# The right-hand end of SBUF at 229280 instead of 229344 in an encoder layer with windowed attention and a SwiGLU feed-forward

## The chip, the cores and the metric

The kernel runs on one core of a Trainium2 chip. The metric is the device time of one execution in microseconds; the time before is the median of three runs.

The core has five engines with queues of their own: TensorE (PE, with its weight loads listed as PEld), VectorE (DVE), ScalarE (ACT), GpSimd (POOL) and SyncE (SP), which here issues nearly all DMAs. SBUF holds the operands, 128 partitions wide; an address below is a byte offset within each partition. PSUM holds the matmul results in eight banks.

## What is computed

One layer (`DEPTH = 1`) of a bidirectional encoder on a 2048 x 1024 sequence in float32: windowed grouped-query attention with 16 query and 4 key heads, then a SwiGLU feed-forward part of 2816 hidden columns. Both are wrapped in norms and in shift, scale and gate vectors that come from a conditioning vector `c`:

```python
mod = (c_act @ ada_w[i] + ada_b[i])[:, None, :]
sh1, sc1, g1, sh2, sc2, g2 = jnp.split(mod, 6, axis=-1)
h = rmsnorm(x, mix_norm_pre[i]) * (1.0 + sc1) + sh1
y = windowed_gqa_sink(h, att_w_qkv[j], att_w_o[j], att_sink[j], rel_bias)
x = x + g1 * rmsnorm(y, mix_norm_post[i])
h = rmsnorm(x, ffn_norm_pre[i]) * (1.0 + sc2) + sh2
y = swiglu(h, ffn_w_in[i], ffn_w_out[i])
x = x + g2 * rmsnorm(y, ffn_norm_post[i])
```

## The kernel before

**Arithmetic.** Every large product is taken as three matmuls (`three`): an operand is split into a rounded half `hi` (a copy to the type fp32r, on ACT) and a rest `lo` (a subtraction, on DVE or POOL), and hi x hi, hi x lo and lo x hi are added up in one PSUM bank. A moving operand has 512 columns in most of these matmuls, the loaded one 128 x 128.

**Stages.** First the modulation products (`ada_reduce`, DVE, each over a 512 KB tile of `ada_w`) together with the first chunk's norm and the query, key and value products of 512 tokens at a time. Then attention in 64 units of a 128-query block and a key head: scores, softmax in the tiles `pr`, transposes by PE with the identity matrix (`ident`), and values. The remaining query, key and value products and the output projections (`OProj`) are woven in between the units. The last chunk's output projection follows by itself. Then come the two products of the feed-forward part. Both use a scheme with seven block products for a 2 x 2 block product (`Block.STEPS`): seven combinations of weights (`a11, s2, a12, s3, s1, a22, s4`) are multiplied with seven operands (`b11, t2, b21, t3, t1, t4, b22`). In the first part (`Hidden`, 44 blocks of seven steps with 12 matmuls each) the blocks' weights take turns between two pools, `wi0` and `wi1`. In the second part (`Outs`) most steps have nine matmuls. The end of the second part is done without the scheme, with operands `gls` and weights `wl`. In the trace `ht...` are operands whose name begins with t, `hb...` those that begin with b, `wa_i` and `ws_i` the weights of the first part, `wa_o` and `ws_o` those of the second.

**Order.** The program is not written straight to the chip. `Recorder` records about 15,700 operations with the buffers they read and write. `place` then gives each pool an address. Pools opened with `side="left"` are stacked upwards from `SBUF_LEFT = 1152`, those with `side="right"` downwards from `SBUF_RIGHT`, and a closed pool gives its room to the next on its side. `forward` and `backward` plan the order of each engine by fixed costs and choose a buffer for each tile. Addresses enter the plan only through `t.earlier` and `t.later`, the lists of earlier buffers whose bytes a buffer overlaps. `emit` issues the planned order with the planned addresses.

**Where the operands lie.** The two sides of the main pools:

| pool | side | bytes from | holds |
|---|---|---|---|
| const | left | 1152 | `mod`, `nsink`, `ones`, `ident` |
| xs, nrm, hs, ev | left | 2560 | activations of the query, key and value products, conditioning row `cb` |
| constr | right | 228864 | `adab`, `gains`, `epsc`, `coef`: 192 + 128 + 32 + 128 bytes |
| w2, raws, w1 | right | 110080 | their weights, raw and split; the `ada_w` tiles |
| bp, qkv, ptp, ob, ws, sm | right | 124160 | attention: bias, q, k, v, phi, plo, output, woven weights |
| pp | right | 105632 | softmax tiles `pr`, three buffers of 6176 bytes |
| op, yp | left | 2560 | output projection of chunks 0 to 2: operands, results |
| op3, wop3, yp3 | right | 148992 | the same for chunk 3, with its weights |
| wi0, hA, b21, t3 | left | 2560 | first part: half of the blocks' weights, operands b11, t2, b21, t3, t1 |
| wi1, hB, tmp | right | 128512 | first part: the other blocks' weights, operands t4, b22, hidden values |
| wo, hA2, tmpo | left | 2560 | second part: all weights, operands b11, t2 |
| hB2, y3 | right | 89600 | second part: operands b21, t3, t1, t4, b22, running sums `z` |

The tiles are 2048 or 4096 bytes in most pools. Those of attention are 1024 to 8192, the weights of the second part 1536 to 6144; all of these are multiples of 256. Not so are the small constants and statistics and `pr`: a buffer of `pr` holds four heads of 385 numbers, 1540 bytes apart.

**Lines.** All operations are issued at line 586 (`emit`), so the profile tells them apart by tile names. The change is in line 68.

Of the kernel before, what the change touches and what calls it, by code (L numbers as in the profile page):

```python
# [64 lines left out]


SBUF_LEFT = 1152
SBUF_RIGHT = 229344
BANKS = 8
BANK = 2048  # L70

# [58 lines left out]
class Recorder:  # L130
# [139 lines left out]
    def place(self):  # L270


        at = {"left": SBUF_LEFT, "right": SBUF_RIGHT, "psum": 0}
        stack = {k: [] for k in at}
# [1379 lines left out]
```

## Time and profile before

| | us |
|---|---|
| median of three runs | 2086.82 |
| lowest and highest run | 2083.96, 2087.82 |
| the profiled execution | 2096.39 |
| its span, first to last instruction | 2094.6 |
| PE busy in it | 2012.7 |
| DVE busy | 1649.6 |
| ACT busy | 1069.9 |
| POOL busy | 755.9 |

The profiled execution is one execution with the profiler on. Its rows add up to its own time, not to the median. A row of a group of instructions gives the engine, the operation, the tiles written and read (out<-in; for a matmul the moving operand first, the loaded one second), the shapes, the count, then busy us and mean ns of one, and the idle time before them with what ended it. Matmuls overlap with their successors, so the time from one start to the next is shorter than the mean of one. The share of DMA is the mean busy share of the core's 16 DMA engines.

### The profile page before, as it was taken

The page shows a single profiled execution, that of the slowest core. Times are in us where ns is not written, and L with a number is a line of the kernel's source. Part 1 is how long each engine was busy: PE and PEld are TensorE (multiplying, and loading weights), DVE is VectorE, ACT ScalarE, POOL GpSimd, SP SyncE. Part 2 cuts the span into 40 slices and gives each one's busy share as a digit, 9 for nine tenths or more (in the row PEclk, how much of TensorE's full clock was granted, in tenths as well). Part 3 has the DMA queues.
Part 4 walks back from the last instruction along what each step waited for, and adds up shares of the span by engine and source line. Part 5 has one row for each costly group of instructions (what it writes and reads, how often), then busy time and mean ns, then how long its engine had stood idle before and what let it go on. Part 6 is the DMA issues. An engine that isn't in the chain of part 4 may idle for free. (4 is left out here: it accounts for less than half of the span.)

```text
span 2094.6 us, 29028 instructions
## 1 busy us (share of the span) xinstructions
PE 2012.7 (96%) x9366; PEld 1664.9 (79%) x9366; DVE 1649.6 (79%) x2933; ACT 1069.9 (51%) x2122; POOL 755.9 (36%) x687
## 2 busy tenths in 40 slices
PE   5899999999999989999999999999999999998997
PEld 4687788888778768888888888888888888876886
DVE  7657777765557879977788897786666789998998
ACT  4447666677777865343433442233333744465432
POOL 2403544456888823543454332222221000240040
PEclk9999999999999999999999999999999999999999
DMA  8887755676768695545456844432233544447553
GB/s 298 266 274 238 234 180 187 209 234 230 237 226 279 207 351 187 187 137 172 158 156 212 288 148 164 133 126 101 94 108 121 181 153 139 146 129 246 168 163 106
DMA packets 200516, 396.35 MB, mean 189 GB/s; under 512 B 20091, under 2 KB 62124, under 8 KB 195244
## 3 DMA queue, kind: packets, MB, share of 16 engines
q1 hardware_dynamic: 199788, 393.97, 56.3%
q8 instruction: 74, 1.21, 0.2%
q14 instruction: 78, 0.64, 0.1%
q10 hardware_dynamic: 576, 0.52, 0.1%
HBM read 270.65 MB, written 123.76 MB: 188 GB/s over the span
## 5 line engine op out<-in xcount | busy, mean ns | idle before, releaser
L586 PE MATMUL bank<-ht,ws_i 128*128 128x512 f32 x1584 | 373.5, 389 | 0.0
L586 PEld LDWEIGHTS bank<-ht,ws_i 128*128 128x128 f32 x1584 | 297.2, 188 | 62.1 <-DVE p_i L586 0.5
L586 PE MATMUL bank<-hb,wa_i 128*128 128x512 f32 x1056 | 253.6, 389 | 0.7 <-DVE u_i L586 0.7
L586 PEld LDWEIGHTS bank<-hb,wa_i 128*128 128x128 f32 x1056 | 198.0, 188 | 42.7 <-DVE u_i L586 1.6
L586 PE MATMUL bank<-ol,wo 128*128 128x512 f32 x768 | 210.7, 403 | 6.1 <-ACT ol L586 4.3
L586 POOL TENSOR_SCALAR pr<-pr,rs 128x384 f32<-128x384 f32 (+1 forms) x256 | 156.8, 629 | 140.7 <-DVE rs L586 140.7
L586 ACT ACTIVATE pr<-pr,nm 128x385 f32<-128x385 f32 (+1 forms) x256 | 155.3, 608 | 82.7 <-DVE nm L586 78.0
L586 POOL TENSOR_TENSOR z<-z,z 128x512 f32<-128x512 f32 x32 | 65.3, 2061 | 345.4 <-DVE z L586 182.2
L586 DVE CUSTOM_DVE_ANT_0 pr<-bank,bias,nsink 128x384 f32<-128x384 f32 (+1 forms) x256 | 147.6, 595 | 51.4 <-PE bank L586 49.7
L586 POOL TENSOR_TENSOR p_i<-p_i,u_i 128x512 f32<-128x512 f32 x44 | 73.7, 1676 | 274.6 <-DVE u_i L586 142.3
L586 PEld LDWEIGHTS bank<-ol,wo 128*128 128x128 f32 x768 | 144.2, 191 | 34.9 <-ACT ol L586 5.1
L586 DVE TENSOR_TENSOR u_i<-bank,u_i 128x512 f32<-128x512 f32 x176 | 120.5, 684 | 45.5 <-PE bank L586 45.5
L586 DVE TENSOR_TENSOR plo<-bank,phi 128x512 fp32r<-128x512 f32 x184 | 119.2, 685 | 36.6 <-ACT phi L586 35.1
L586 PE MATMUL bank<-k,q 128*128 128x384 f32 (+1 forms) x512 | 133.2, 346 | 6.7 <-DVE nm L586 6.6
L586 ACT CAST ws_i<-s_i 128x512 fp32r<-128x512 f32 x132 | 81.8, 620 | 107.8 <-PE bank L586 93.3
L586 PE MATMUL bank<-hi,ws 128*128 128x512 f32 x384 | 135.8, 402 | 0.1
L586 DVE TENSOR_TENSOR wa_i<-wiri,wa_i 128x512 fp32r<-128x512 f32 x132 | 111.4, 845 | 29.4 <-ACT wa_i L586 29.2
L586 ACT CAST wa_i<-wiri 128x512 fp32r<-128x512 f32 x132 | 81.8, 620 | 91.4 <-PE bank L586 91.4
L586 PE MATMUL bank<-ht,wa_i 128*128 128x512 f32 x528 | 126.8, 389 | 0.0
L586 PE MATMUL bank<-hb,ws_i 128*128 128x512 f32 x528 | 126.8, 389 | 0.0
L586 DVE TENSOR_TENSOR ws_i<-s_i,ws_i 128x512 fp32r<-128x512 f32 x132 | 115.0, 871 | 3.9 <-ACT ws_i L586 3.9
L586 PE MATMUL bank<-hi,w 128*128 128x512 f32 x320 | 103.4, 402 | 14.4 <-ACT hi L586 14.4
(245 smaller groups left out, 4515.2 us busy)
## 6 DMA issues: line engine op xcount, KB each, us to landing
wiri<-w_in SPq DMA_DIRECT2D x88, 512.0 KB, 4.9
ada<-ada_w SPq DMA_DIRECT2D x40, 512.0 KB, 5.1
wiro<-w_out SPq DMA_DIRECT2D x48, 384.0 KB, 3.7
q_d<-e SPq DMA_DIRECT2D x64, 256.0 KB, 4.3
q<-q_d SPq DMA_DIRECT2D x16, 1024.0 KB, 6.2
wo<-wo_d SPq DMA_DIRECT2D x16, 1024.0 KB, 6.8
g_d_b<-p_i SPq DMA_DIRECT2D x44, 256.0 KB, 5.5
g_d_t<-p_i SPq DMA_DIRECT2D x40, 256.0 KB, 2.0
```

The costliest lines, as they stand in the source:

```text
L586: getattr(engs[o.eng], o.fn)(*args, **kw)
```

## The change

One constant is lowered by 64. `place` counts the right-hand stack from it, so each right-hand tile of the program stands 64 bytes lower: 228864, where the right-hand operands end, becomes 228800. Left-hand tiles, PSUM, the DRAM tensors, tile sizes and all code stay.

```diff
 SBUF_LEFT = 1152
-SBUF_RIGHT = 229344
+SBUF_RIGHT = 229280
 BANKS = 8
 BANK = 2048
```

## The prediction

> **What bounds the kernel now.** I read the page's first and fourth parts, then the busy time by stretches, then the groups of PE.
>
> ```profile
> span 2094.6 us, 29028 instructions
> PE 2012.7 (96%) x9366; PEld 1664.9 (79%) x9366; DVE 1649.6 (79%) x2933; ACT 1069.9 (51%) x2122; POOL 755.9 (36%) x687
> ...
> q1 hardware_dynamic: 199788, 393.97, 56.3%
> ...
> HBM read 270.65 MB, written 123.76 MB: 188 GB/s over the span
> ...
> PE 30%; DVE 4%; DMA 3%; issue 2%; ACT 1%; POOL 0%; SPq 0%; DVEq 0%; ACTq 0%; POOLq 0%
> ```
>
> PE is busy 96% of the span, so 2094.6 - 2012.7 = 81.9 us are left in which PE has nothing. The chain of waits is followed only as far back as where its shares end (they add to some 40%). On it DMA landings hold 3%, 62.8 us. The stretches show where PE is idle, and beside what:
>
> ```profile
> 0.00:20.00 20.00, 6.20 (x6) 1.50 (x6) 9.04 (x13) 12.55 (x16) 2.77 (x7) 1.00 0.90 328
> 20.00:50.00 30.00, 22.18 (x85) 18.15 (x86) 28.30 (x40) 12.75 (x18) 12.35 (x5) 1.00 0.87 283
> 50.00:80.00 30.00, 25.21 (x125) 20.37 (x125) 18.44 (x22) 13.60 (x21) 18.87 (x12) 1.00 0.72 222
> 80.00:130.00 50.00, 44.68 (x247) 39.04 (x248) 36.47 (x63) 24.07 (x47) 8.69 (x6) 0.90 0.82 283
> ...
> 730.00:800.00 70.00, 63.93 (x269) 50.37 (x268) 54.61 (x72) 44.94 (x75) 17.87 (x11) 0.98 0.92 339
> ...
> 840.00:1260.00 420.00, 420.00 (x1854) 347.79 (x1853) 357.82 (x481) 173.83 (x293) 177.23 (x117) 1.00 0.55 182
> ...
> 1880.00:1920.00 40.00, 32.12 (x113) 23.56 (x114) 33.30 (x57) 22.82 (x42) 0.00 (x0) 0.87 0.74 249
> ```
>
> The columns are: length, busy time and count of PE, PEld, DVE, ACT and POOL, granted clock, share of the DMA engines, GB/s. From 840 to 1260 us PE never stops: 420.00 us / 1854 = 226.5 ns per matmul, and nothing but the matmul's own pace counts. The idle time with busy DMA engines lies in the other six: 13.8 + 7.8 + 4.8 + 5.3 + 6.1 + 7.9 = 45.7 us.
>
> **The change part by part.** No instruction, tile size, queue or order is written anew. Every right-hand address falls by 64.
>
> *Which operands move.* The right-hand constants take 480 bytes, so the right-hand operands now end at 229344 - 480 = 228864 = 894 x 256, remainder 0. The left-hand ones begin at 1152 + 1408 = 2560, also remainder 0. All larger tiles but the softmax's are multiples of 256 bytes, so all start at 0 today. Afterwards the right-hand ones start at 192 and the left-hand ones stay at 0.
>
> *Order and room: nothing.* The planner uses addresses for one thing, which earlier buffers a new buffer overlaps. Both sides' slots are in coarse steps: the right-hand hidden-sum tiles (89600 upwards, step 2048) have their borders 1024 from those of the left-hand operands they follow, and the softmax tiles start 608 above the last left-hand byte under them. With right-hand addresses 64 lower, the 1,584 pairs of buffers that share bytes are the same pairs. The tightest room, in the first feed-forward part, is 128512 - 127488 = 1024 bytes. So the instruction order stays, and I take 0. Were a pair to appear, a first write would wait for a last read. That is a rival below.
>
> *Loads of weights, and DVE, ACT and POOL: nothing.* The softmax tiles `pr` already start at other remainders: the buffers at 160, 192 and 224, their heads 4 bytes further each. They can be laid beside `vt`, which starts at 0:
>
> ```profile
> L586 PEld LDWEIGHTS bank<-ident,pr x736: 137/141/230, 192.2 to 729.7; 128*128 128x128 f32 x184
> ...
> L586 ACT ACTIVATE pr<-pr,nm x256: 494/618/674, 184.3 to 716.1; 128x385 f32<-128x385 f32 x112, 128x257 f32<-128x257 f32 x16
> ```
>
> ```profile
> L586 PEld LDWEIGHTS bank<-ident,vt x16: 138/140/143, 235.0 to 277.1; 128*128 128x128 f32 x16
> ```
>
> ```profile
> L586 PEld LDWEIGHTS bank<-ident,pr 128*128 128x128 f32 x736 | 90.9, 141 | 10.4 <-POOL pr L586 0.8 <-DVE plo L586 0.3
> ```
>
> The first two fences give minimum, median and maximum in ns, the third busy us and mean ns. The loaded operand is named second, so `pr` is what PE loads: median and mean 141 ns, against 140 for `vt`. Were the one buffer in three that stands at exactly 192 slower by x, the mean would lie x/3 above. The bounds for an ACT instruction are the ends of its row, which mix two widths; I take 0. The two-input DVE work that would newly mix sides is small, chiefly the 40 modulation products:
>
> ```profile
> L586 DVE CUSTOM_DVE_ANT_0 ada<-ada,cb,adab 128x1024 f32<-128x1024 f32 x40 | 58.1, 1459 | 10.5 <-DMA ada<-ada_w 9.3 <-DMA adab<-ada_b 1.2
> ```
>
> Sixteen of these come before PE is fed, in the stretch where DVE is busy 28.30 of 30 us. 10% more on each would be 16 x 0.15 = 2.3 us; its row gives no sign of it, and I take 0.
>
> *The moving operand of a matmul: unknown, taken as 0.* No moving operand stands off remainder 0 today. After the change 3,672 of them do: k (512), phi and plo (368), the last output projection (192), v tiles (192), two of seven steps in the first feed-forward part (44 x 2 x 12 = 1,056), five of seven in the second (1,200), half of the 288 at the end, and 8 in the norms. The price of a column comes from two rows:
>
> ```profile
> L586 PE MATMUL bank<-gls,wl 128*128 128x256 f32 x192 | 24.1, 286 | 0.0
> L586 PE MATMUL bank<-gls,wl 128*128 128x512 f32 x96 | 21.9, 389 | 0.0
> ```
>
> (389 - 286) / 256 = 0.40 ns. Lower bound 0. Upper bound: one more 256-byte piece, 64 columns, 25.8 ns, times 3,672 = 95 us. The nearest row is the load of `pr`, another read of SBUF by PE, and it shows no difference, so 0 is taken. [...]
>
> *Transfers: +5.0 us.* By the tile sizes 176.8 of the 270.65 MB read go to the right-hand side and 74.7 of the 123.76 written come from it: 251.5 / 394.4 = 64%. Most of these move 2,048 bytes a partition. Such a row covers eight 256-byte blocks at remainder 0, and nine at 192. A packet now takes 0.563 x 16 x 2094.6 us / 199788 = 94.4 ns on the mean for 1,972 bytes, so a ninth piece costs between 0 and 12 ns, 1/8. Lower bound: 0, since all DMA lies beside PE's work. Upper bound: the DMA time of the six stretches, 18.0 + 26.1 + 21.6 + 41.0 + 64.4 + 29.6 = 200.7 us, x 0.64 / 8 = 16 us. I take the part on the chain: 62.8 x 0.64 / 8 = 5.0 us, as what is not on the chain has cover (SP's queue is ahead, PE at 100% in 840 to 1260). A load that comes later delays the DVE and ACT splits, then the first matmul of its block. The direct cost to PE is small today:
>
> ```profile
> PE bank L586 <- DMA x_d<-y: 1.4, 1, 1.4
> ```
>
> [...] No run here shows a right-hand row at 192.
>
> **Sum.** The profiled execution took 2096.39 us, 1.8 more than its span. 2096.39 + 0 + 0 + 0 + 5.0 = 2101.4, that is +0.24%. The median of the runs is 2086.82, 9.6 us under the profiled one, so on it: 2086.82 x 1.0024 = 2091.8, rounded to 2092. Its own range, from the bounds 0 and 16: 2087 to 2103, and 2 us lower for the spread of the runs.
>
> **The rivals.**
>
> *Hidden anyway.* The extra pieces cost nothing, or fall beside work. For it: PE waits 1.4 us in all for a DMA directly, and in the first 50 us DVE is the fuller engine. Against it: the DMA share of 0.92 in 730 to 800, where PE stands 6.1 us. Time 2087, no change.
>
> *Moving operands pay.* Each of the 3,672 loses the 64 bytes of its broken first piece, 16 columns, 6.4 ns: 23.5 us, 2110. For it: only loads, not moving operands, are shown at other remainders. Against it: `pr`. It decides from about 1.1 ns a matmul, where 3,672 of them exceed 4.2 us.
>
> *The other side: two reads of PE get out of each other's way.* Today the load and the moving operand run at the same remainder. 5,024 matmuls have them on different sides (3,096 with right-hand weights, 1,928 with left-hand). Of the 226.5 ns some 512 x 0.40 = 206 go by columns, so 20.5 do not, and these are the bound of what a clash can hold: 103 us in all. I price an eighth of it, one 256-byte piece in the eight of a row, 2.6 ns: 5,024 x 2.6 = 13 us go, 2074. For it: the fixed part is there in every pairing. Against it: nothing today differs between pairings, but all are at equal remainders, so that tells little. It decides from 0.8 ns a matmul.
>
> *The change doesn't do only what it says.* The planner could come to another order after all, by a pair of buffers I did not see: either sign, a few us.
>
> **How the numbers follow.** A measurement of this kernel tells about 0.2% (4.2 us) from no change. Forecast 0.40; of its range 0 to 16 us, 0.31 lies over 4.2 and 0.09 under. Hidden 0.20 (0.18 no change, 0.01 to each side). Moving operands 0.17, slower. Reads apart 0.19, faster. Another order 0.04 (0.01 faster, 0.02, 0.01). Sum: faster 0.21, same 0.29, slower 0.50. The range runs from 2074, the price of the faster rival, to 2112, just above that of the moving operands; what is left out is the far half of either.
>
> **What would show it.** Right: packets' share of q1 rises from 56.3% with the same 199788 packets, the landings of right-hand loads grow while left-hand ones stay, the six stretches grow by 3 to 10 us together, and 420 us still hold 1854 matmuls. The weights' loads stay at 188 and 141 ns. Wrong: a share of 56.3% and the same landings (hidden); steps with `t4` and `b22` at another pace than the five others of a block (moving operands); blocks with left-hand and right-hand weights at different paces, under 226.5 ns (reads apart); another count or order of instructions on an engine.

## The result, and the profile after

The kernel after took 2110.48 us (median of four runs, 2109.34 to 2113.78), the kernel before 2087.13 us beside it (2083.96 to 2087.82). The ratio is 1.0112, with a 95% interval of 1.0095 to 1.0129: slower by 1.1%, 23.4 us. Every engine issues the same instructions in the same order as before. The page of the profiled execution (2109.34 us):

```profile
span 2107.6 us, 29028 instructions
PE 2034.4 (97%) x9366; PEld 1666.3 (79%) x9366; DVE 1648.1 (78%) x2933; ACT 1077.8 (51%) x2122; POOL 758.9 (36%) x687
...
q1 hardware_dynamic: 199788, 393.97, 55.7%
```

PE is busy 2034.4 - 2012.7 = 21.7 us longer with the same 9,366 matmuls; DVE, ACT and POOL hardly move. The queue's share fell, 56.3% to 55.7%, with the same packets. So PE itself is slower, and not because it waits. The stretches, with the columns of the prediction, say where:

```profile
0.00:20.00 20.00, 6.20 (x6) 1.50 (x6) 9.28 (x15) 12.63 (x16) 2.78 (x7) 1.00 0.91 333
20.00:50.00 30.00, 22.64 (x87) 18.41 (x88) 28.30 (x38) 12.70 (x18) 12.51 (x5) 1.00 0.87 287
50.00:80.00 30.00, 24.85 (x123) 19.78 (x122) 18.06 (x22) 13.59 (x21) 18.66 (x11) 1.00 0.69 214
80.00:130.00 50.00, 44.50 (x240) 38.86 (x241) 35.20 (x62) 23.67 (x47) 9.62 (x6) 0.86 0.83 283
130.00:180.00 50.00, 50.00 (x220) 41.05 (x219) 23.42 (x42) 24.18 (x45) 4.53 (x6) 1.00 0.88 293
...
730.00:800.00 70.00, 64.29 (x270) 50.93 (x269) 55.26 (x71) 45.15 (x74) 17.24 (x10) 0.98 0.90 331
...
840.00:1260.00 420.00, 420.00 (x1824) 342.75 (x1824) 352.74 (x479) 173.83 (x288) 175.29 (x115) 1.00 0.54 181
...
1880.00:1920.00 40.00, 32.68 (x127) 24.82 (x126) 32.63 (x53) 25.35 (x49) 11.23 (x6) 0.91 0.60 197
```

In the six stretches where PE waits beside DMA it stands 13.8 + 7.4 + 5.2 + 5.5 + 5.7 + 7.3 = 44.9 us, against 45.7 before. From 840 to 1260 us PE is busy throughout at a granted clock of 1.00, as before, but 420 us hold 1,824 matmuls instead of 1,854: 230.3 ns each against 226.5. In the one earlier stretch in which PE never stops, 130 to 180 us, it is 220 matmuls instead of the 222 of before:

```profile
130.00:180.00 50.00, 50.00 (x222) 41.39 (x221) 24.02 (x43) 24.34 (x45) 5.57 (x7) 1.00 0.90 297
```

The timeline of PE shows which matmuls are slow. A row merges neighbouring matmuls by tile names: start, us, then the names and the count. A matmul overlaps the next (one of the first part lasts 389 ns on the mean in the kernel before, and the next starts some 227 ns after it), so the pace is the time from one row's start to the next, divided by the count. Before, from operand `t4` of a block with left-hand weights to `t4` of the next block, whose weights are right-hand:

```profile
917.97 2.88 PE L586 MATMUL bank<-ht,wa_i 128*128 128x512 f32 x12
...
937.01 2.20 PE L586 MATMUL bank<-ht,wa_i 128*128 128x512 f32 x9
```

It is (937.01 - 917.97) / 84 = 226.7 ns for every matmul. After, the same blocks, from `b21` on:

```profile
910.04 2.88 PE L586 MATMUL bank<-hb,wa_i 128*128 128x512 f32 x12
...
918.20 2.96 PE L586 MATMUL bank<-ht,wa_i 128*128 128x512 f32 x12
...
923.80 2.96 PE L586 MATMUL bank<-hb,wa_i 128*128 128x512 f32 x12
...
937.80 1.56 PE L586 MATMUL bank<-ht,wa_i 128*128 128x512 f32 x6
```

`b21`, `t3` and `t1` on left-hand weights: (918.20 - 910.04) / 36 = 226.7 ns, as before. `t4` and `b22`, right-hand operands on the same left-hand weights: (923.80 - 918.20) / 24 = 233.3. In the next block the weights are right-hand, and now the five left-hand operands are slow: (937.80 - 923.80) / 60 = 233.3. Its `t4` and `b22`, right-hand on right-hand, fall back to 226.7 after some eight matmuls of 227 to 240 ns. Then the next block begins, with left-hand weights:

```profile
940.56 2.88 PE L586 MATMUL bank<-hb,ws_i 128*128 128x512 f32 x12
943.27 2.92 PE L586 MATMUL bank<-hb,wa_i 128*128 128x512 f32 x12
946.04 2.88 PE L586 MATMUL bank<-ht,ws_i 128*128 128x512 f32 x12
```

Its first twelve, `b11`, take (946.04 - 943.27) / 12 = 230.8 ns (230.2 on the mean over all such blocks), although their remainders are equal, and the twelve of `b22` ahead of them, equal too, ran at 226 to 227. So a change from pairs at 192 to pairs at 0 costs a little as well. These rows suggest that neither being off remainder 0 nor being weights or moving operand is what costs, but that a matmul takes 6.67 ns longer when its two operands lie at different remainders; the experiments test that.

By these paces the first part's 3,696 matmuls cost 3,696 x (230.3 - 226.5) = 14.0 us. In the second part the mean from start to start, over neighbouring matmuls without idle time, rose from 226.67 to 233.33 ns for the 1,200 matmuls with right-hand operands on left-hand weights, and to 227.55 for the other 480: 8.0 + 0.4 us, as far as no wait hides it. Together that is at most 22.4 us of the 23.4.

The rows that answer to the rest of the prediction's are those of the tiles `pr` and `vt`, the modulation products, and the landings (DMA rows: KB each, median us from issue to landing). All but the last two fences are of the kernel after; these two show the landings before and after:

```profile
L586 PEld LDWEIGHTS bank<-ident,pr x736: 137/141/223, 193.5 to 728.2; 128*128 128x128 f32 x184
...
L586 ACT ACTIVATE pr<-pr,nm x256: 495/618/668, 185.6 to 714.6; 128x385 f32<-128x385 f32 x112, 128x257 f32<-128x257 f32 x16
```

```profile
L586 PEld LDWEIGHTS bank<-ident,vt x16: 138/140/142, 236.4 to 276.6; 128*128 128x128 f32 x16
```

```profile
L586 DVE CUSTOM_DVE_ANT_0 ada<-ada,cb,adab 128x1024 f32<-128x1024 f32 x40 | 56.7, 1422 | 10.0 <-DMA ada<-ada_w 8.5 <-DMA adab<-ada_b 1.3
```

```profile
wiri<-w_in SPq DMA_DIRECT2D x88, 512.0 KB, 4.9
...
ht4o<-g_d_t SPq DMA_DIRECT2D x20, 256.0 KB, 4.2
```

```profile
wiri<-w_in SPq DMA_DIRECT2D x88, 512.0 KB, 4.8
...
ht4o<-g_d_t SPq DMA_DIRECT2D x20, 256.0 KB, 4.0
```

Loads of weights (141 ns for `pr`, 140 for `vt`), ACT (618 ns), DVE (1422 ns for 1459) and landings (4.8 us for 4.9, 4.0 for 4.2) stayed where they were.

### The profile page after: what moved, and what is told of

Its sections match the earlier page's. It is cut to its first block, busy times and chain, and to the rows that moved or that the text cites. A ratio compares the mean times of both kernels' runs of the same rounds, so it can differ in the third digit from the quotient of the medians.

```text
span 2107.6 us, 29028 instructions
## 1 busy us (share of the span) xinstructions
PE 2034.4 (97%) x9366; PEld 1666.3 (79%) x9366; DVE 1648.1 (78%) x2933; ACT 1077.8 (51%) x2122; POOL 758.9 (36%) x687
## 3 DMA queue, kind: packets, MB, share of 16 engines
q1 hardware_dynamic: 199788, 393.97, 55.7%
## 4 chain that ended last, share of the span: by engine, by line
PE 79%; DMA 7%; DVE 6%; issue 3%; ACT 2%; POOL 2%; SPq 1%; DVEq 0%; ACTq 0%; POOLq 0%
PE bank L586 79%; DVE z L586 1%; DMA ada<-ada_w 1%; POOL y L586 1%; DMA zx<-x_d 1%; SPq L586 1%; DMA hd_d_t<-hf 1%; DMA out<-zx 1%; DMA wqkv<-w_qkv 1%; DMA hb21o<-g_d_b 1%; DVE ada L586 0%; POOL pr L586 0%; DVE zx L586 0%; DVE ws_o L586 0%; DMA gains<-gains 0%
## 5 line engine op out<-in xcount | busy, mean ns | idle before, releaser
L586 PE MATMUL bank<-ht,ws_i 128*128 128x512 f32 x1584 | 378.5, 393 | 0.0
L586 DVE TENSOR_TENSOR z<-bank,z 128x512 f32<-128x512 f32 (+1 forms) x164 | 107.3, 658 | 13.8 <-PE bank L586 13.5
```

Source lines behind the costliest of these rows:

```text
L586: getattr(engs[o.eng], o.fn)(*args, **kw)
```

## The experiments

Remainders are modulo 256, and a difference is the moving operand's remainder less the loaded one's, modulo 256. The kernel before, measured beside the runs, had medians of 2090.65 us (19 runs, for the first four experiments), 2090.89 (7 runs, for the next four) and 2093.18 (one run, for the last four), and each experiment is compared with its own.

**The kernel before, profiled again.** No edit.

> The kernel before once more, for a second profile: the first one took 2096.39 us where the median of its runs is 2087. Pairs theory (a matmul is 6.7 ns slower when its loaded and its moving operand start at different remainders modulo 256): all 512-column matmuls of the feed-forward parts at 226.7 ns from start to start, about 2087 us, and the 9 us that the first profile had more lie in the stages that wait, not in the pace of PE. Rival: the pace itself varies between executions, so that some groups stand above 227 ns.

One run of 2086.83 us. Its span, 2085.0 us, is 9.6 us less than that of the first profile of the same kernel.

```profile
730.00:800.00 70.00, 65.40 (x276) 51.98 (x276) 56.74 (x76) 46.46 (x77) 14.67 (x8) 0.98 0.85 315
840.00:1260.00 420.00, 420.00 (x1855) 347.87 (x1854) 357.38 (x481) 172.45 (x289) 179.25 (x117) 1.00 0.54 184
```

From 840 to 1260 us it is the same to one matmul (x1855 to x1854), while 730 to 800 holds 276 for 269. So differences of some us in the waiting stages mean nothing here, and the feed-forward pace is exact. This span, 2085.0, is the better one to set against 2107.6. Where the 22.6 us between them lie is told by the first and last starts of the feed-forward parts (rows: ns of one, minimum, median and maximum, then first to last start in us), here and in the kernel after:

```profile
L586 PE MATMUL bank<-hb,wa_i x1056: 388/389/390, 783.7 to 1612.1; 128*128 128x512 f32 x176
...
L586 PE MATMUL bank<-hb11o,wa_o x240: 388/389/409, 1623.2 to 1998.0; 128*128 128x512 f32 x120
...
L586 PE MATMUL bank<-hb22o,ws_o x240: 388/389/391, 1632.8 to 2021.3; 128*128 128x512 f32 x120
```

```profile
L586 PE MATMUL bank<-hb,wa_i x1056: 387/396/398, 787.4 to 1629.6; 128*128 128x512 f32 x176
...
L586 PE MATMUL bank<-hb11o,wa_o x240: 387/389/496, 1640.9 to 2020.7; 128*128 128x512 f32 x120
...
L586 PE MATMUL bank<-hb22o,ws_o x240: 393/394/398, 1649.8 to 2044.6; 128*128 128x512 f32 x120
```

The first part grew from 1623.2 - 783.7 = 839.5 to 1640.9 - 787.4 = 853.5 us, by the 14.0 that its pace says. The second grew from 398.1 to 403.7, by 5.6 of the 8.4 that its pace says. There PE had waits that shrank: from 1630 to 1880 us it stands 3.9 us here and 0.2 in the kernel after. Ahead of the first part 3.7 us were added, after the second 0.7 taken away. The 3.7 can't be told from the spread of these stages, as the first profile of the kernel before reached the first part only at 789.2.

**Both sides at remainder 192.** The sides are equal again, and every large operand and its DMA rows lie off the boundary (16 of `mod`'s 80 columns, which nothing uses, go).

```diff
-SBUF_RIGHT = 229344
+SBUF_RIGHT = 229280
...
-    mod = const.tile([P, 80], F32, name="mod")
+    mod = const.tile([P, 64], F32, name="mod")
```

> Both sides at remainder 192: the right-hand end at 229280 as in the change, and the left-hand operands 64 bytes lower too (mod has 64 columns instead of 80, of which 48 are used). Pairs theory: loaded and moving operand stand at the same remainder again in every pair, so 226.7 ns everywhere and the time of before, 2087 us (ratio 1.000 within 0.002). Boundary theory (operands that don't start on a 256-byte boundary pay, in PE or in the pieces of a DMA row): now every operand and every DMA row is off the boundary, so at least the 23 us of the change and up to about 23 x 1.5 = 35 us: 2110 to 2122 us.

2093.0 us (10 runs), ratio 1.0014 (1.0005 to 1.0024). Its queues and the timeline of PE:

```profile
q1 hardware_dynamic: 199788, 393.97, 56.6%
```

```profile
907.25 2.88 PE L586 MATMUL bank<-hb,wa_i 128*128 128x512 f32 x12
...
934.45 2.88 PE L586 MATMUL bank<-ht,wa_i 128*128 128x512 f32 x12
```

(934.45 - 907.25) / 120 = 226.7 ns, over matmuls of all but the one pairing that follows. The pace is back with both operands off the boundary, so a boundary that one operand misses isn't the cause. The ratio leaves 1.0 to 5.0 us for all else that remainder 192 does, DMA included, with all large rows moved, where the change moved those of the right-hand side (64% of the bytes by the prediction's count). The DMA engines' time, 0.566 x 2089.7 = 1182.8 us each, is 0.6% over 0.564 x 2085.0 = 1175.9 of the kernel before's second profile and 0.3% over its first.

**Only the left side at 192.** The mirror of the change.

```diff
-    mod = const.tile([P, 80], F32, name="mod")
+    mod = const.tile([P, 64], F32, name="mod")
```

> The left-hand operands alone 64 bytes lower (remainder 192), the right-hand end as before (remainder 0). Pairs theory: the same 5,024 pairs stand 64 bytes apart, only the sign is turned, so the time of the change, 2110 us (ratio about 1.011), with 233.3 ns in the pairs of different sides and 226.7 in the others. Boundary theory for moving operands: the left-hand moving operands pay instead of the right-hand ones, so left-hand weights with left-hand moving operands would be slow; DMA theory: the left-hand 36% of the traffic pays instead of 64%, about half the loss, 2098 us.

2105.85 us (4 runs), ratio 1.0076 (1.0059 to 1.0093). The stretch from 130 to 180 us, where left-hand operands run on right-hand weights and PE never stops, and the timeline of PE, `t4` first:

```profile
130.00:180.00 50.00, 50.00 (x216) 40.19 (x215) 23.49 (x42) 23.65 (x45) 4.36 (x6) 1.00 0.88 292
```

```profile
920.05 2.93 PE L586 MATMUL bank<-ht,wa_i 128*128 128x512 f32 x12
...
925.57 2.95 PE L586 MATMUL bank<-hb,wa_i 128*128 128x512 f32 x12
928.36 2.96 PE L586 MATMUL bank<-ht,ws_i 128*128 128x512 f32 x12
...
933.96 5.29 PE L586 MATMUL bank<-ht,ws_i 128*128 128x512 f32 x22
```

So the matmuls ahead of the feed-forward parts pay too: 216 in this stretch for 222 before, and 222 x 226.7 / 233.3 is 215.7. Left-hand operands on right-hand weights again take (933.96 - 928.36) / 24 = 233.3 ns. But right-hand operands on left-hand weights take only (925.57 - 920.05) / 24 = 230.0. Their difference is 64, that of the others 192. So the difference counts, and 64 seemed cheaper; yet in the kernel after, the 60 matmuls at 233.3 on right-hand weights have difference 64 too. That had to be settled.

**The right side 256, 128, 192 and 32 bytes lower than before.** One constant each:

```diff
-SBUF_RIGHT = 229344
+SBUF_RIGHT = 229088   # right side at 0
+SBUF_RIGHT = 229216   # at 128
+SBUF_RIGHT = 229152   # at 64
+SBUF_RIGHT = 229312   # at 224
```

> The right-hand end 256 bytes lower than before (229088): another address, the same remainder. Pairs theory with modulus 256 or a divisor of it: 226.7 ns in all pairs and 2087 us (ratio 1.000 within 0.002). Rival, that the distance itself matters, or that a larger modulus does (512 or more): the pairs of different sides are slow again, 233 ns, about 2110 us.

> The right-hand end 128 bytes lower than before (229216, remainder 128). Pairs theory with modulus 256: the pairs of different sides are slow; if the price is fixed, 233.3 ns and 2110 us again; if it grows with the distance (16 cycles for 64 bytes), 32 cycles, 240 ns, and about 2135 us. Modulus 128 or 64 x 2: no pair is slow, 226.7 ns, 2087 us.

> The right-hand end 192 bytes lower (229152, remainder 64): the pairs stand 64 bytes apart with the other sign, as in the run with the left side lowered, but with the left-hand operands at 0. If the sign decides, the pace is that run's: about 233.2 ns for right-hand weights with left-hand moving operands and about 229 to 230 for left-hand weights with right-hand moving ones, and some 2106 us. If only the distance decides, 233.3 ns in both kinds and 2110 us. If the price grows with the distance counted downwards, 48 cycles, 246 ns, and some 2160 us.

> The right-hand end 32 bytes lower (229312, remainder 224). Fixed price for any difference: 233.3 ns in the pairs of different sides, 2110 us. Price by distance: 8 cycles, 230.0 ns, about 2098 us. A step of 64 bytes, so that 32 don't matter: 226.7 ns, 2087 us.

The prices by distance in these expectations are estimates from the 6.67 ns that 64 bytes cost in the kernel after: twice that makes 240 ns, three times some 246, half 230. No run shows the length of a cycle.

| right side at | us (runs) | ratio, interval |
|---|---|---|
| 0, 256 lower | 2090.4 (10) | 1.000, 0.999 to 1.001 |
| 128 | 2105.7 (4) | 1.0068, 1.0053 to 1.0083 |
| 64, 192 lower | 2108.51 (4) | 1.0080, 1.0063 to 1.0096 |
| 224, 32 lower | 2112.24 (4) | 1.0101, 1.0086 to 1.0116 |

A whole 256 costs nothing. Moving the right side to 64 gives the paces of the left side at 192 to the hundredth (229.85 and 233.20, table below), so only the difference of the sides counts. And 32 bytes already cost the whole price:

```profile
910.42 2.88 PE L586 MATMUL bank<-hb,wa_i 128*128 128x512 f32 x12
...
918.58 2.96 PE L586 MATMUL bank<-ht,wa_i 128*128 128x512 f32 x12
...
938.18 1.09 PE L586 MATMUL bank<-ht,wa_i 128*128 128x512 f32 x4
```

Left on left (918.58 - 910.42) / 36 = 226.7 ns, then 84 mixed ones (938.18 - 918.58) / 84 = 233.3: a step of 32 bytes isn't free for PE, it costs 6.6 ns here.

One thing doesn't fit. At 128 the mixed pairs are as slow as after the change, which by the way of summing above makes 21 us, but the runs show 11 to 17. The missing us aren't in the feed-forward parts: in its profile the first takes 1636.7 - 784.3 = 852.4 us and the second 2041.9 - 1636.7 = 405.2, against 853.5 and 403.7 in the kernel after. They may lie in the stages ahead of the first, which end between 783.7 and 794.0 us in the traces of all runs; where they ended in the runs of the kernel before that this one is compared with isn't on record.

**A difference within the left side.** An unused tile of 64 bytes in pool `wi0` moves b11, t2, b21, t3 and t1 of the first part to 64 and nothing else.

```diff
+    wi[0].tile([P, 16], F32, name="gap")
```

> The right-hand end as before, and in the first feed-forward part alone an unused tile of 64 bytes between the left-hand weights and the left-hand operands (b11, t2, b21, t3, t1 start at remainder 64; both sides' weights and t4, b22 at 0). The planner's order changes somewhat with it, so the pace of PE is what is compared, not the whole time. Pairs theory: now the pairs within the left side are slow, 229 to 233 ns, and so are right-hand weights with left-hand moving operands; right-hand moving operands run at 226.7 ns with weights of either side. A theory in which the two ends of SBUF or the distance between them matter: left-hand weights with left-hand moving operands stay at 226.7 ns.

One run: 2100.25 us. The timeline of PE from `b21` of a block with left-hand weights:

```profile
907.47 2.91 PE L586 MATMUL bank<-hb,wa_i 128*128 128x512 f32 x12
...
915.71 2.91 PE L586 MATMUL bank<-ht,wa_i 128*128 128x512 f32 x12
...
921.18 2.93 PE L586 MATMUL bank<-hb,wa_i 128*128 128x512 f32 x12
...
934.93 2.93 PE L586 MATMUL bank<-ht,wa_i 128*128 128x512 f32 x12
```

Left on left, slow for the first time: (915.71 - 907.47) / 36 = 228.9 ns; left on right (934.93 - 921.18) / 60 = 229.2, the same. So it isn't the two sides either. `t4` and `b22`, at equal remainders, come down to 226 and 227 ns only after five to ten matmuls in the trace. The second part, which the gap doesn't touch, stays at 226.67.

**The weights alone off.** The change, with 192 more bytes above `t4` and `b22` in `hB`, so that they lie at 0 and only the right-hand weights of the first part at 192. Every mixed pair there now has difference 64, and no pair of another difference comes before it.

```diff
 SBUF_RIGHT = 229280
...
+    hB.tile([P, 48], F32, name="gap", bufs=1)
```

> The change (right-hand end at 229280), and in the first feed-forward part an unused tile of 192 bytes above t4 and b22, so that these start at remainder 0 again, as do the left-hand weights and operands; the right-hand weights alone stand at 192. The planner's order differs somewhat, so the pace of PE is compared. In the changed kernel the pairs of right-hand weights with left-hand moving operands (moving minus loaded = 64) ran at 233.1 ns, but in the run with the left side lowered pairs with the same difference of 64 ran at 229 to 230. History theory: which of the two it is depends on the pace that the matmuls before had; here all blocks with left-hand weights run at 226.7, so the right-hand ones follow a block at 226.7 and run at about 229. Place theory (the side of the weights decides): 233 ns as in the changed kernel. Pairs theory in both: left-hand weights with t4 and b22 are at 226.7 again, and right-hand weights with t4 and b22 are slow for the first time.

One run: 2098.28 us. The timeline of PE:

```profile
915.42 2.88 PE L586 MATMUL bank<-ht,wa_i 128*128 128x512 f32 x12
...
920.86 2.91 PE L586 MATMUL bank<-hb,wa_i 128*128 128x512 f32 x12
...
934.59 2.91 PE L586 MATMUL bank<-ht,wa_i 128*128 128x512 f32 x12
```

`t4` and `b22` on left-hand weights are at 226.7 ns ((920.86 - 915.42) / 24), and the 60 left-hand operands on right-hand weights at (934.59 - 920.86) / 60 = 228.8. Those are the pairs that take 233.3 in the kernel after, with the same weights and operands at the same remainders. What differs is what runs before: here pairs at 226.7, there 24 pairs of difference 192 at 233.3. So difference 64 costs 2.2 ns by itself and goes on at 233.3 where pairs at that pace come first.

The kernel after shows the same within one trace. Two of its blocks, one with left-hand and one with right-hand weights, take turns step by step, so that each twelve matmuls of left-hand operands on right-hand weights come behind twelve on left-hand weights, at equal remainders:

```profile
1182.04 5.63 PE L586 MATMUL bank<-ht,ws_i 128*128 128x512 f32 x24
...
1203.90 5.71 PE L586 MATMUL bank<-ht,wa_i 128*128 128x512 f32 x24
```

The 96 matmuls take (1203.90 - 1182.04) / 96 = 227.7 ns. Half of them, the equal pairs, run at 226.7, so the pairs 64 apart take some 228.7 here, and 233.3 in the blocks beside, where they follow pairs 192 apart. The 220 matmuls from 130 to 180 us fit in: all but two of them are left-hand operands on right-hand weights, 64 apart, with no pair 192 apart among them, and 222 x 226.7 / 228.9 is 219.9.

**The remaining steps of 32.**

```diff
-SBUF_RIGHT = 229344
+SBUF_RIGHT = 229248   # right side at 160
+SBUF_RIGHT = 229120   # at 32
+SBUF_RIGHT = 229184   # at 96
```

> Right-hand end 96 bytes lower (229248, remainder 160): moving minus loaded is 160 for left-hand weights with right-hand moving operands, 96 the other way round. Fixed price for most differences: 233 ns in both kinds, about 2105 to 2112 us. If the differences below 128 are cheaper, the second kind stands below the first.

> Right-hand end 224 bytes lower (229120, remainder 32): differences 32 and 224, those of the 32-byte run with the kinds exchanged. If the difference alone decides: 233.2 to 233.4 ns in both kinds, about 2110 us. If history decides at 32: below 233 ns for left-hand weights with right-hand moving operands, which follow pairs at 226.7.

> Right-hand end 160 bytes lower (229184, remainder 96): differences 96 and 160, those of the 96-byte run with the kinds exchanged. Fixed price: 233 ns in both kinds, about 2105 to 2112 us; a difference of 96 that follows pairs at 226.7 could be cheaper, as 64 was (229 ns). No difference runs below 226.7 ns by the pairs theory.

2112.70, 2114.09 and 2113.82 us, one run each. The paces of the first part, as the mean time from one start to the next over neighbouring 512-column matmuls without idle time (some 400 and 1,080 of a pairing in each trace):

| left, right side at | right-hand operand on left-hand weights: difference, ns | left-hand operand on right-hand weights: difference, ns |
|---|---|---|
| 0, 0 (before) | 0, 226.67 | 0, 226.67 |
| 192, 192 | 0, 226.67 | 0, 226.66 |
| 0, 192 (after) | 192, 233.32 | 64, 233.09 |
| 192, 0 | 64, 229.85 | 192, 233.20 |
| 0, 64 | 64, 229.85 | 192, 233.20 |
| 0, 128 | 128, 232.96 | 128, 233.26 |
| 0, 224 | 224, 233.44 | 32, 233.24 |
| 0, 32 | 32, 233.41 | 224, 233.22 |
| 0, 160 | 160, 234.01 | 96, 233.31 |
| 0, 96 | 96, 233.64 | 160, 234.05 |

All but 0 and 64 cost 6.3 to 7.4 ns, and no pairing of 512 columns ran below 226.66 on the mean. No layout that was tried beats the kernel before.

## Why the prediction was right or wrong

The time fell into the range and on the side that was named likeliest, but not by the forecast's way: the 5.0 us for transfers didn't show, and most of the 23.4 us came from the term that was taken as 0. As to the forecast, the number was met by luck.

*Which operands move; order and room: nothing.* Right. The order is the same on each engine.

*Loads of weights, and DVE, ACT and POOL: nothing.* Right. The load of `pr` stayed at 141 ns, of `vt` at 140; the modulation products took 1422 ns for 1459.

*The moving operand of a matmul: unknown, taken as 0.* This is the step that failed. "The nearest row is the load of `pr`, another read of SBUF by PE, and it shows no difference" looked at the duration of a load by itself. The price is a matter of both operands, and shows in the pace of the matmuls. That every 512-column pair ran at one pace before could not tell, since all had a difference of 0. The set was wrong too. Of the 3,672 operands that moved, the 528 on right-hand weights in the first part (44 / 2 x 2 x 12) kept 226.7 ns but for the eight or so at the start of each such run (228.3 on the mean). The 1,320 left-hand operands on right-hand weights, which hadn't moved, paid: their weights had.

*Transfers: +5.0 us.* Too large, and not seen in the trace. The queue's share went from 56.3% to 55.7%, landings didn't grow, the six stretches have 44.9 us of idle PE for 45.7. With all large operands at 192 the whole kernel was 1.0 to 5.0 us slower, and this holds all that rows off the boundary do, those of the left-hand side included; 64% of it would be 0.6 to 3.2 us, an estimate. The term took an eighth of a packet's time for a ninth piece. Pieces of 256 bytes, in which the bound of 25.8 ns and the price of 2.6 ns are counted too, were the author's estimate. No run shows them, nor the term: with all large operands at 192 the DMA engines' time was 0.3% to 0.6% above that of the kernel before.

*Sum and range.* The profiled 2096.39 us was itself 9.6 above the median; the second profile shows that this lay in the stages that wait and not in the pace, so carrying a ratio over to the median was harmless. The range held the result because it reached to the rival of the moving operands.

*Hidden anyway.* For the transfers this was nearest to what was seen, but the time went up for another reason.

*Moving operands pay.* Its 2110 hits the time by 3,672 x 6.4 ns = 23.5 us. The price was near, 6.67, the set was not: the mixed pairs of the feed-forward parts are 528 + 1,320 + 1,200 = 3,048. At a mean of some 6.5 ns they make 19.8 us, and those of equal remainders that run slower behind a change 2.3 more; of these 22.1 us, the starts above leave some 19.6 after waits. That both ways give 2110 is chance.

*Two reads of PE get out of each other's way.* It counted the right set, the 5,024 matmuls with their operands on different sides, and named the right thing to look at, the relation of the two reads. The sign was the other one: equal remainders are the fast case. Of the 5,024 the 3,048 of the feed-forward scheme make nearly all of the loss. The other 1,976 don't go free, but lie mostly in stages where PE waits: from 130 to 180 us, where it doesn't, 220 matmuls were done for 222, and 216 with the left side at 192. At the end of the second part the 96 matmuls of `gls` with 512 columns went from 226.7 to 231.2 ns on the mean, half of them with operands on different sides. The 192 with 256 columns lost nothing (143 in a row take 17.64 us, and 17.72 in the second profile of before).

*What would show it.* Of the signs of the forecast only one appeared, the unchanged loads of weights: the share fell, the landings and the six stretches stayed, and 420 us held 1,824 matmuls. The sign given for moving operands, `t4` and `b22` at another pace than the five others, did appear in each block. Which of the two groups was slow changed with the side of the weights, and that spoke for the pair.

Open are: why PE takes longer, and whether the loaded operand that counts is a matmul's own or the next one's, which PE loads beside it (loads of weights are busy for 342.75 of the 420 us in which PE never stops; in the long runs both lie alike); steps under 32 bytes; why 256 columns lose nothing; what carries the slow pace over to difference 64, and what slows equal pairs behind a change; and the 4 to 10 us that the runs at 128 lack.

## What to carry to other kernels

Give the loaded and the moving operands of 512-column matmuls the same remainder modulo 256 in SBUF (226.67 ns from start to start here, and 233.0 to 234.1 at most differences): allocators that stack from two ends need the constants of both ends padded alike. A change of 64 bytes in a small constant tile (`mod`) moved every large operand behind it and took the time from 2090.65 to 2105.85 us, so when all matmuls of a long stretch slow by a few ns, look at addresses. Measure the pace from start to start, sorted by the pairing of operands. The loads' means don't show it (188 to 192 ns in the feed-forward parts before, 187 to 192 after), and the means of single matmuls show it only in groups of one pairing: `ht1o,ws_o`, right-hand on left-hand, went from 389 to 396 ns and `hb11o,wa_o`, left-hand on left-hand, from 390 to 391, while `ht,ws_i`, which mixes them, went from 389 to 393.

## What was not expected of the hardware

- 512-column matmuls went from 226.67 to some 233.3 ns (233.0 to 234.1), 2.9%, when loaded and moving operand started 32, 96, 128, 160, 192 or 224 bytes apart modulo 256, and to some 229 ns at 64. Those with 256 columns showed no loss (17.64 us for 143, 17.72 before).
- The price doesn't grow with the distance (233.41 ns at 32, 232.96 at 128, 233.44 at 224). It is not tied to the boundary (both at 192: 226.67), nor to SBUF's two ends (both on the left, 64 apart: 228.9).
- The pace depends on what ran before: up to ten matmuls of equal remainders took 224 to 240 ns behind matmuls at other remainders, even where those were equal and at 226 to 227 themselves (`b11` at 0 behind `b22` at 192, 230.2 on the mean of twelve), and pairs 64 apart stayed at 233.3 for 60 matmuls behind a slow run, where they took 228.7 to 229.9 behind a fast one.
- Rows that start at 192 instead of 0 cost DMA little: with all of them so, 0.3% to 0.6% of the engines' time.
